# Copying a finished background product out of PSUM on VectorE instead of ScalarE, in the scan of a bidirectional SSD block

## The chip, the cores and the metric

One of the cores of a Trainium2 chip runs the whole program. The metric is the device time of one execution in microseconds (us). Engines are named as in the profile: PE (TensorE, matmul), PEld (its weight loads), DVE (VectorE), ACT (ScalarE), POOL (GpSimd), SP (SyncE, which here only issues DMAs). Names such as L553 are lines of the kernel.

## The reference, cut to what matters

The reference is one encoder block over 1024 tokens and 16 meta tokens, model width 1024, all in float32. The part that bears on the change:

```
u = rmsnorm(h) @ w_in                      # g_val, g_gate, z, x, B, C, dt, gate_conv, gate_ssm
y_conv = silu(layernorm(dwconv(g_val * sigmoid(g_gate)))) @ conv_out_w
y_fwd  = ssd_chunked(x, dt_f, a_f, B, C)             # 4 groups x 8 heads of 64, state 128, chunks of 128 tokens
y_bwd  = flip(ssd_chunked(flip(x), flip(dt_b), a_b, flip(B), flip(C)))
y_ssm  = gated_rmsnorm(y_fwd + y_bwd + d * x, z) @ ssm_out_w
h = h + (sigmoid(gate_conv) * y_conv + sigmoid(gate_ssm) * y_ssm) @ w_o
h = h + (silu(rmsnorm(h) @ w_gate) * (rmsnorm(h) @ w_up)) @ w_down
```

Three products in it don't belong to the scan itself, but are computed while the scan runs: the columns `gate_conv` and `gate_ssm` of `u`, and the first half (rows 0 to 1023) of the product with `ssm_out_w`.

## The kernel before

Every float32 operand of a large product is split in two rounded parts, high and low, and a product is three matmuls per 128 rows of the inner dimension (`mm3_parts`, L201 to L208). Weights are loaded by SP, rounded on ACT (L138) and their low part is made on POOL or DVE (L139), two tiles ahead.

The program has four stages: projections and convolutions (to about 694 us), the scan (about 694 to 1270 us), the remaining products with `ssm_out_w`, `conv_out_w` and `w_o`, and the feed-forward block.

**The scan.** For each of the 4 groups a backward pass (`backward`, L706) makes transposed tiles and the backward states, and 8 forward chunks (`class Chunk`, L750) make the output of 128 tokens each, 32 chunks in all. A string of letters, `SEQ` (L41, used at L909), fixes the order of the steps of three neighbouring chunks: L loads and computes `cb` (L775 to L781), s/S and t/T make the decay masks and their exponentials in two halves of four heads (`select`, `scores`), D, O and C make the outputs and carry the state, M adds and multiplies by the gate (`gated`, L856), N, P and V square, scale and store. Within a chunk the data goes round the engines: DVE masks `cb` (L777, L778), ACT scales it by dt (`gg`, L788), DVE adds the backward part (L790), PE makes the mask sums `ss`, ACT their exponential (`e`, L810), DVE multiplies (L811), PE multiplies by x, DVE adds up (`y`, L843, L849, L860) and multiplies by the gate (L861), ACT squares that (`sz`, L866), POOL makes the root (`rs`), ACT scales (L870).

**The background.** The digits in `SEQ` put background work between these steps (`step_bg`, L665): the generator `background` (L640) first runs 8 blocks of `gate_block` (L544), each of 4 tiles of 128x512, then loads the first half of the normed scan output (`load_vn`, L613: DMA, then ACT `oph` L622, then DVE `opl` L623), and then 16 tiles of the first half of the `ssm_out_w` product. A tile takes 24 matmuls, cut in three pieces (`PARTS`, L37), so that scan steps fit between them. When the last of the 24 is done, the tile is copied from PSUM to the SBUF tile `w512` (two buffers, in the trace `w`): by L553 for the gate blocks and by L656 for the product. SP stores it in DRAM (L554, L657). There are 32 + 16 = 48 such copies.

**The bank.** All matmul outputs of the scan share 8 PSUM banks (`PSB`, L588). At first background tiles rotate over three banks (`mm`, `ss`, `yd`); from step 18 of the first backward pass on (L883, L884) they have the one bank `mm`. From there the first matmul of a background tile can only start when the copy of the tile before has read that bank.

**What sets the order.** Each engine works through its own queue in order. PE's order in the scan is exactly that of the program text (`strict`, `tie`, L187). The order on DVE, ACT, POOL and SP is decided by the framework's scheduler when the program is built.

Of the kernel before, what the change touches and what calls it, by code (L numbers as in the profile page):

```python
# [57 lines left out]
def tile_hybrid_block(  # L58
# [7 lines left out]
    V, S, GP, PE, SP = nc.vector, nc.scalar, nc.gpsimd, nc.tensor, nc.sync  # L66
    x = x[0]
    out = out[0]
# [73 lines left out]
    def next_w(key):  # L142

        while plan and len(ready) < 2:
            k, view, lo = plan.pop(0)
            ready.append((k, load_w(view, lo)))
        k, w = ready.pop(0)
        assert k == key, (k, key)
        return w
# [106 lines left out]
    def proj(wh, wl, j, spans, ps_of=None):  # L256
        for t0, n in spans:
            ps = (ps_of or ps_mm)()
            yield from mm3_parts(ps[:, :n], [wh[:, k, j * P:(j + 1) * P] for k in range(KC)],
                                 [wl[:, k, j * P:(j + 1) * P] for k in range(KC)],  # L260
                                 [h[:, t0:t0 + n] for h in hnh], [h[:, t0:t0 + n] for h in hnl],
                                 PARTS if ps_of else ())
            yield t0, n, ps

    def z_block(b, pool, ps_of, pool_w=2):
        wh, wl = next_w(f"z{b}")
        for i in range(NTT):
            ps = ps_of()
            sl = slice(NM + i * P, NM + (i + 1) * P)
            for k in range(KC):  # L270
                for q_, (a, bb) in enumerate(((hnh[k], wh), (hnh[k], wl), (hnl[k], wh))):
                    PE.matmul(ps[:, :256], lhsT=a[:, sl], rhs=bb[:, k, :], start=(k == 0 and q_ == 0),  # L272
                              stop=(k == KC - 1 and q_ == 2))
            zt = pool.tile([P, 512], F32, name="w512", tag="w512", bufs=pool_w)[:, :256]
            S.activation(out=zt, in_=ps[:, :256], func=AF.Silu)  # L275
            S.dma_start(out=d_sz[b // 2][i, :, (b % 2) * 256:(b % 2 + 1) * 256], in_=zt)
            yield
# [266 lines left out]
    def gate_block(key, b, dst, pool, ps_of, pool_w=2):  # L544
        w = next_w(f"{key}{b}")
        for j in range(2):
            for done in proj(*w, j, SPAN_R, ps_of):
                if done is None:
                    yield
                    continue  # L550
                t0, n, ps = done
                gt = pool.tile([P, 512], F32, name="w512", tag="w512", bufs=pool_w)
                S.copy(out=gt, in_=ps)  # L553
                SP.dma_start(out=dst[2 * b + j, :, t0 - NM:t0 - NM + n], in_=gt)  # L554
                yield

# [39 lines left out]
    def pc():  # L596
        return pb(next(ps_ring))
# [15 lines left out]
    def load_vn(kh):  # L613

        op = []
        for hh in range(2):
            for k in range(KC):
                raw = wts.tile([P, 1024], F32, name="wraw", tag="wraw", bufs=2)[:, :512]
                SP.dma_start(out=raw, in_=d_vn[2 * kh + k // 4][:, k % 4, hh * 512:(hh + 1) * 512])
                h, l = op_tile()  # L620
                w = prm(R_SN, KC * kh + k)
                S.activation(out=h, in_=raw, func=AF.Copy, scale=w)  # L622
                V.scalar_tensor_tensor(out=l, in0=raw, scalar=w, in1=h.bitcast(F32), op0=ALU.mult, op1=ALU.subtract)  # L623
                op.append((h, l))
        return op

    def gemm(op, key, ps_of, parts=()):

        for b in range(4):
            wh, wl = next_w(f"{key}{b}")  # L630
            for hh in range(2):
                for j in range(2):
                    js = slice(j * P, (j + 1) * P)
                    ps = ps_of()
                    yield from mm3_parts(ps, [wh[:, k, js] for k in range(KC)], [wl[:, k, js] for k in range(KC)],
                                         [t[0] for t in op[hh * KC:(hh + 1) * KC]],
                                         [t[1] for t in op[hh * KC:(hh + 1) * KC]], parts)
                    yield 2 * b + j, hh, ps

    def background():  # L640
        for k, i in BGP:
            if k == "z":
                yield from z_block(i, sd, ps_bg, 2)
            else:
                yield from gate_block(k, i, d_gc if k == "gc" else d_gs, sd, ps_bg)
        hn_ctx.close()
        opp_box.append(ctx.enter_context(tc.tile_pool(name="ops", bufs=16, side="right")))
        op = load_vn(0)
        yield
        for done in gemm(op, "s0", ps_bg, PARTS):  # L650
            if done is None:
                yield
                continue
            i, hh, ps = done
            pt = sd.tile([P, 512], F32, name="w512", tag="w512", bufs=2)
            S.copy(out=pt, in_=ps)  # L656
            SP.dma_start(out=d_p[i, :, hh * 512:(hh + 1) * 512], in_=pt)  # L657
            yield

    ps_bg = lambda: pb(next(bg_ring[0]))  # L660
    bg = background()
    bg_acc = [0.0]
    strict[0] = True
# [231 lines left out]
    for f in range(NCK + 1):  # L895
# [3 lines left out]
        if f % NTT == 0:  # L899
# [8 lines left out]
            V=lambda: old and old.store(), b=ahead, e=extra)  # L908
# [16 lines left out]
    def gate(src, i, ts):  # L925
        gt = mg.tile([P, 512], F32, name="mgt", bufs=3)
        SP.dma_start(out=gt, in_=src[i, :, ts])
        S.activation(out=gt, in_=gt, func=AF.Sigmoid)
        return gt
# [64 lines left out]
    for n_, (i, hh, ps) in enumerate(gemm(op, "s1", pc)):  # L994
        ts = halves(hh)
        gt = gate(d_gs, i, ts)
# [7 lines left out]
    for i, hh, ps in gemm(op, "c", pc):  # L1004
        ts = halves(hh)
        gt = gate(d_gc, i, ts)
# [41 lines left out]
    for b in range(4):  # L1048
        wh, wl = next_w(f"o{b}")
        for i in range(NTT):  # L1050
            ps = pc()
# [131 lines left out]
```

## Time and profile before

| what | value |
|---|---|
| time, median of 3 runs | 2297.45 us (2295.74 to 2298.12) |
| time of the profiled execution | 2297.74 us |
| its span, first to last instruction | 2295.9 us |
| mean granted TensorE clock | 0.991 of 2.4 GHz |
| busy over the whole span: PE, DVE, ACT, POOL | 97%, 60%, 33%, 37% |

The profiled execution lies 0.29 us above the median; 1.84 us of its time lie outside its span. A share of busy time is a mean over stages with different limits, so the stage of the scan is read by itself, in stretches of the trace. In a timeline a row is: start in us, duration in us, engine, line, operation, output<-inputs, shapes, count, and in brackets the idle time of that engine before it and what ended it. "PE mm L196 <- ACT w L553" means that a matmul of PE that writes the bank `mm` sat waiting for ACT's copy `w` of L553.

### The profile page before, as it was taken

The page shows a single profiled execution, that of the slowest core. Times are in us where ns is not written, and L with a number is a line of the kernel's source. Part 1 is how long each engine was busy: PE and PEld are TensorE (multiplying, and loading weights), DVE is VectorE, ACT ScalarE, POOL GpSimd, SP SyncE. Part 2 cuts the span into 40 slices and gives each one's busy share as a digit, 9 for nine tenths or more (in the row PEclk, how much of TensorE's full clock was granted, in tenths as well). Part 3 has the DMA queues.
Part 4 walks back from the last instruction along what each step waited for, and adds up shares of the span by engine and source line. Part 5 has one row for each costly group of instructions (what it writes and reads, how often), then busy time and mean ns, then how long its engine had stood idle before and what let it go on. Part 6 is the DMA issues. An engine that isn't in the chain of part 4 may idle for free.

```text
span 2295.9 us, 30987 instructions
## 1 busy us (share of the span) xinstructions
PE 2228.8 (97%) x12103; PEld 1903.6 (83%) x12103; DVE 1383.9 (60%) x1726; ACT 764.4 (33%) x1386; POOL 846.0 (37%) x729
## 2 busy tenths in 40 slices
PE   7999999999999999988999999999999999999998
PEld 7999999999997766665677788998888888888886
DVE  4389898997871587887997664533332333433236
ACT  6333342322322454545555462223111111111112
POOL 3374664821202586867785510111010110101102
PEclk9999999999999999999999999999999999999999
DMA  4222222232236675746753752411111111111111
GB/s 140 85 76 67 83 70 71 86 119 99 89 109 202 195 209 164 226 142 209 229 169 119 241 159 84 147 38 52 41 56 37 55 39 53 55 37 56 37 55 73
DMA packets 223162, 245.29 MB, mean 107 GB/s; under 512 B 19113, under 2 KB 174361, under 8 KB 223017
## 3 DMA queue, kind: packets, MB, share of 16 engines
q1 hardware_dynamic: 210200, 221.89, 31.3%
q10 hardware_dynamic: 12816, 21.44, 2.5%
q8 instruction: 95, 1.56, 0.3%
q14 instruction: 51, 0.41, 0.1%
HBM read 174.23 MB, written 69.04 MB: 106 GB/s over the span
## 4 chain that ended last, share of the span: by engine, by line
PE 48%; DMA 2%; DVE 2%; ACT 1%; POOL 1%; issue 1%; SPq 0%; POOLq 0%; DVEq 0%; ACTq 0%
PE yo L196 11%; PE mm L196 9%; PE ss L196 4%; PE yd L196 4%; PE cb L196 4%; PE yo L1107 3%; PE ss L1107 2%; PE cb L1107 2%; PE yd L1107 2%; DMA wraw<-d_vn 1%; PE mm L1107 1%; PE yo L1058 1%; PE cb L1058 1%; PE ss L1058 1%; PE mm L1058 1%
## 5 line engine op out<-in xcount | busy, mean ns | idle before, releaser
L139 POOL TENSOR_TENSOR wl<-wraw,wh 128x1024 fp32r<-128x1024 f32 (+1 forms) x103 | 249.9, 2436 | 1080.0 <-ACT wh L138 1079.8
L196 PE MATMUL mm<-hnh,wh 128*128 128x352 f32 (+4 forms) x1208 | 410.6, 340 | 14.9 <-ACT w L553 13.5
L196 PE MATMUL mm<-hnh,wl 128*128 128x352 f32 (+4 forms) x1208 | 403.8, 334 | 2.8 <-POOL wl L139 2.8
L196 PE MATMUL mm<-hnl,wh 128*128 128x352 f32 (+4 forms) x1208 | 405.8, 336 | 0.4 <-DVE hnl L378 0.4
L138 ACT CAST wh<-wraw 128x1024 fp32r<-128x1024 f32 (+1 forms) x172 | 175.0, 1042 | 420.3 <-PE yd L1107 175.5
L139 DVE TENSOR_TENSOR wl<-wraw,wh 128x1024 fp32r<-128x1024 f32 x69 | 139.2, 2020 | 252.6 <-ACT wh L138 247.8
L196 PEld LDWEIGHTS mm<-hnh,wh 128*128 128x128 f32 x1208 | 228.3, 189 | 29.9 <-ACT w L553 17.5
L474 DVE SCALAR_TENSOR_TENSOR acc<-ap,pr,acc 128x1024 f32<-128x1024 f32 x192 | 247.5, 1289 | 6.3
L196 PEld LDWEIGHTS mm<-hnh,wl 128*128 128x128 f32 x1208 | 228.3, 189 | 12.9 <-POOL wl L139 3.4
L196 PEld LDWEIGHTS mm<-hnl,wh 128*128 128x128 f32 x1208 | 228.2, 189 | 9.8 <-issue 1.2
L474 DVE SCALAR_TENSOR_TENSOR acc<-xp,pr,acc 128x1040 f32<-128x1040 f32 x120 | 156.6, 1305 | 4.0
L196 PE MATMUL mm<-oph,wh 128*128 128x512 f32 x344 | 139.5, 405 | 11.9 <-ACT w L656 9.9
L272 PE MATMUL mm<-wh,hnh 128*128 128x256 f32 x512 | 144.7, 283 | 5.1 <-ACT w L275 5.1
L272 PE MATMUL mm<-wl,hnh 128*128 128x256 f32 x512 | 144.6, 283 | 0.0
L272 PE MATMUL mm<-wh,hnl 128*128 128x256 f32 x512 | 144.5, 283 | 0.0
L196 PE MATMUL mm<-opl,wh 128*128 128x512 f32 x344 | 137.1, 398 | 3.0 <-DVE opl L623 3.0
L196 PE MATMUL yo<-oph,wh 128*128 128x512 f32 x352 | 139.0, 395 | 0.0
L196 PE MATMUL yo<-opl,wh 128*128 128x512 f32 x352 | 138.9, 395 | 0.0
L196 PE MATMUL yo<-oph,wl 128*128 128x512 f32 x352 | 138.8, 394 | 0.0
L196 PE MATMUL mm<-oph,wl 128*128 128x512 f32 x344 | 136.7, 397 | 0.0
L758 POOL TENSOR_SCALAR_AFFINE_SELECT sel<-adh 128x512 fp32r<-128x512 f32 x128 | 98.7, 792 | 70.8 <-ACT wh L138 41.6
L513 POOL TENSOR_TENSOR tap<-tap 128x1024 f32<-128x1024 f32 x40 | 96.1, 2403 | 34.4 <-ACT tap L509 33.3
(316 smaller groups left out, 4938.8 us busy)
## 6 DMA issues: line engine op xcount, KB each, us to landing
wraw<-in_w_in_dram SPq DMA_DIRECT2D x72, 512.0 KB, 3.7
xc<-d_x SPq DMA_DIRECT2D x64, 256.0 KB, 3.5
wraw<-in_w_gate_dram SPq DMA_DIRECT2D x22, 512.0 KB, 4.7
wraw<-in_w_up_dram SPq DMA_DIRECT2D x22, 512.0 KB, 3.8
wraw<-in_w_down_dram SPq DMA_DIRECT2D x22, 512.0 KB, 3.7
d_x<-xa ACTq DMA_DIRECT2D x16, 520.0 KB, 2.6
d_sz<-w ACTq DMA_DIRECT2D x64, 128.0 KB, 2.1
d_xt<-xt SPq DMA_DIRECT2D x32, 256.0 KB, 3.3
```

The lines of the kernel that those rows point to most:

```text
L138: S.copy(out=h3[:, sl], in_=r3)
L139: (V if lo[i] == "v" else GP).tensor_tensor(out=l3[:, sl], in0=r3, in1=h3[:, sl].bitcast(F32), op=ALU.subtract)
L196: tie(PE.matmul(out_, **kw))
L272: PE.matmul(ps[:, :256], lhsT=a[:, sl], rhs=bb[:, k, :], start=(k == 0 and q_ == 0), stop=(k == KC - 1 and q_ == 2))
L474: V.scalar_tensor_tensor(out=out_ if last else acc, in0=sl(k), scalar=w(k), in1=acc, op0=ALU.mult, op1=ALU.add)
L513: GP.tensor_tensor(out=t, in0=t, in1=part, op=ALU.add)
L758: GP.affine_select(out=dst, in_=hbc(src, self.c, h0, 4, P, P), pattern=[[0, 4], [-1 if back else 1, P]], compare_op=ALU.is_ge, fill=0.0, b ...
L1058: PE.matmul(ps[:, :256], lhsT=a[:, sl], rhs=bb[:, k, :], start=(k == 0 and q_ == 0), stop=(k == KC - 1 and q_ == 2))
L1107: PE.matmul(ps, lhsT=a[:, sl], rhs=bb[:, k, t0:t0 + n], start=(k == 0 and q_ == 0), stop=(k == 1 and q_ == 2))
```

## The change

The two copies move from the queue of ACT to that of DVE. What they copy, the number of copies, the buffers, the DMAs and the order of the matmuls in the scan stay.

```diff
@@ gate_block @@
                 gt = pool.tile([P, 512], F32, name="w512", tag="w512", bufs=pool_w)
-                S.copy(out=gt, in_=ps)
+                V.tensor_copy(out=gt, in_=ps)
                 SP.dma_start(out=dst[2 * b + j, :, t0 - NM:t0 - NM + n], in_=gt)
@@ background @@
             pt = sd.tile([P, 512], F32, name="w512", tag="w512", bufs=2)
-            S.copy(out=pt, in_=ps)
+            V.tensor_copy(out=pt, in_=ps)
             SP.dma_start(out=d_p[i, :, hh * 512:(hh + 1) * 512], in_=pt)
```

Where the scheduler puts them is shown at two of the 48 tiles. In the queues the buffers are numbered; `w_8249` is the 18th tile, whose copy starts at 861.55 us in the trace of before, and `w_9542` the 26th, at 971.74 us.

ACT's queue before, around the 18th tile (`sbh` is the rounded backward state, `gg` the weighted mask of the next chunk, `cch` the rounded C, `bt` a transposed B, `e` the exponential):

```order
L685 CAST sbh<-s_bl 128x512
L788 ACTIVATE gg<-cb,dt 128x128 x4
L691 CAST cch<-cc 128x128
L553 COPY w_8249<-mm 128x512
L726 COPY bt<-tp 128x128
L810 ACTIVATE e<-ss 128x512
```

The copy stood behind the second set of four `gg` of ACT and ahead of the exponential.

DVE's queue around the same tile, where the row with + is new (`y` is the backward output, `s_bl` the low part of the backward state, `ccl` the low part of C):

```order
 L849 TENSOR_TENSOR y_8220<-yo,ea 128x512
 L790 SCALAR_TENSOR_TENSOR gg<-cb,dt,gg 128x128 x4
+L553 COPY w_8249<-mm 128x512
 L686 TENSOR_TENSOR s_bl<-s_bl,sbh 128x512
 L692 TENSOR_TENSOR ccl<-cc,cch 128x128
```

The copy now stands behind DVE's own four `gg`, which read what ACT's four `gg` wrote.

DVE's queue around the 26th tile:

```order
 L790 SCALAR_TENSOR_TENSOR gg<-cb,dt,gg 128x128 x4
 L686 TENSOR_TENSOR s_bl<-s_bl,sbh 128x512
+L553 COPY w_9542<-mm 128x512
 L692 TENSOR_TENSOR ccl<-cc,cch 128x128
 L811 TENSOR_TENSOR e<-e,gg 128x512
```

Here it stands one operation further back, behind `s_bl`. On ACT the copy was removed between the same neighbours as above.

## Rows read from the trace of the kernel before

**Rows 1.** Busy time in two stretches of the scan, before and after about 776 us.
```profile
core 0: us, PE busy (x) PEld busy (x) DVE busy (x) ACT busy (x) POOL busy (x), PEclk, DMA share, GB/s
694.00:776.00 82.00, 80.94 (x359) 62.67 (x358) 20.11 (x30) 25.03 (x51) 25.67 (x27) 1.00 0.66 202
776.00:1270.00 494.00, 459.66 (x2342) 336.06 (x2341) 401.18 (x712) 256.40 (x630) 361.40 (x435) 0.98 0.62 185
```

**Rows 2.** Waits, 694 to 1290 us: us in total, times, longest us.
```profile
ACT sz L866 <- DVE y L861: 99.6, 31, 8.8
...
PE mm L196 <- ACT w L553: 13.5, 11, 3.2
...
PE mm L196 <- ACT w L656: 9.9, 7, 3.1
```

**Rows 3.** Groups by form, 694 to 1270 us: busy us, mean ns of one, idle before.
```profile
L553 ACT COPY w<-mm 128x512 f32<-128x512 f32 x27 | 15.9, 589 | 21.2 <-PE mm L196 16.9 <-issue 4.2
L656 ACT COPY w<-mm 128x512 f32<-128x512 f32 x16 | 9.3, 582 | 6.8 <-PE mm L196 6.8
L700 DVE COPY s_b<-yo 128x512 f32<-128x512 f32 x4 | 2.8, 688 | 11.0 <-PE yo L196 11.0
```

**Rows 4.** Timeline around the copy of the 18th tile.
```profile
860.91 0.40 PE L196 MATMUL mm<-hnh,wl 128*128 128x512 f32 x1
...
861.55 0.61 ACT L553 COPY w<-mm 128x512 f32<-128x512 f32 x1
...
862.02 1.11 DVE L790 SCALAR_TENSOR_TENSOR gg<-cb,dt,gg 128x128 f32<-128x128 f32 x4
...
862.21 0.50 PE L196 MATMUL mm<-hnh,wh 128*128 128x512 f32 x1 [0.91 <-ACT w L553]
...
863.06 0.97 DVE L686 TENSOR_TENSOR s_bl<-s_bl,sbh 128x512 fp32r<-128x512 f32 x1
...
864.94 0.60 ACT L810 ACTIVATE e<-ss 128x512 f32<-128x512 f32 x1 [0.66 <-PE ss L196]
...
865.57 1.07 DVE L811 TENSOR_TENSOR e<-e,gg 128x512 f32<-128x512 f32 x1 [1.34 <-ACT e L810]
```

**Rows 5.** Timeline around the copy of the 26th tile.
```profile
970.00 0.39 PE L196 MATMUL mm<-hnh,wl 128*128 128x512 f32 x1
...
970.42 0.68 DVE L843 TENSOR_TENSOR y<-yo,ea 128x512 f32<-128x512 f32 x1
...
971.01 0.68 DVE L811 TENSOR_TENSOR e<-e,gg 128x512 f32<-128x512 f32 x1
...
971.74 0.61 ACT L553 COPY w<-mm 128x512 f32<-128x512 f32 x1
...
972.98 0.48 PE L196 MATMUL mm<-hnh,wh 128*128 128x512 f32 x1
...
973.25 0.96 DVE L686 TENSOR_TENSOR s_bl<-s_bl,sbh 128x512 fp32r<-128x512 f32 x1
```

**Rows 6.** Timeline: the first and the last of the 18 waits for a copy.
```profile
754.26 0.59 ACT L553 COPY w<-mm 128x512 f32<-128x512 f32 x1 [4.19 <-issue]
...
754.90 0.50 PE L196 MATMUL mm<-hnh,wh 128*128 128x512 f32 x1 [0.28 <-ACT w L553]
...
1268.59 0.57 ACT L656 COPY w<-mm 128x512 f32<-128x512 f32 x1
...
1268.71 0.75 DVE L623 SCALAR_TENSOR_TENSOR opl<-wraw,pr,oph 128x512 fp32r<-128x512 f32 x1 [1.57 <-ACT oph L622]
```

**Rows 7.** Timeline: the first and the last of 13 places without a wait.
```profile
788.70 1.53 DVE L811 TENSOR_TENSOR e<-e,gg 128x512 f32<-128x512 f32 x1
...
790.35 0.47 PE L196 MATMUL mm<-hnh,wh 128*128 128x512 f32 x1
...
1260.92 0.75 DVE L623 SCALAR_TENSOR_TENSOR opl<-wraw,pr,oph 128x512 fp32r<-128x512 f32 x1
...
1261.57 0.41 PE L196 MATMUL mm<-oph,wh 128*128 128x512 f32 x1
```

**Rows 8.** Timeline: a wait of PE at 1007 us.
```profile
1007.09 0.84 PE L196 MATMUL yd<-e,xt 128*64 128x128 f32 x8 [2.02 <-DVE e L811]
```

**Rows 9.** Busy time in the stretch behind that wait, columns as in rows 1.
```profile
1007.45:1010.80 3.35, 3.35 (x13) 2.14 (x9) 3.28 (x8) 0.47 (x1) 0.00 (x0) 0.50 0.68 176
```

## The prediction

> **What bounds the kernel now.** I read the busy time in stretches first. From 776 us to the end of the scan PE is busy for 459.66 of 494 us, so it is idle for 34.3 us; before 776 us it loses only 1.06 of 82 us [rows 1]. In the long stretch VectorE is busy for 401.18 us (81%), ScalarE for 256.40 us (52%): the change takes work from the emptier engine and gives it to the fuller one. The list of waits says what PE's idle time is: 13.5 us in 11 waits for the copies of L553 and 9.9 us in 7 waits for those of L656, 23.4 us in all [rows 2]. So two thirds of what PE loses in the scan hang on the instructions that are moved, and when each copy is done decides the time. The timelines around single copies come last: they show what stands ahead of a copy in ScalarE's queue, and where VectorE is at that moment.
>
> **One copy.** On ScalarE it takes 589 or 582 ns; the nearest row on VectorE, a copy of the same shape out of PSUM, 688 ns [rows 3]. A copy that starts at the same time therefore frees its bank 0.10 us later. In VectorE's queue it takes up less than that: where VectorE reads PSUM and the next operation waits for nothing, starts lie 0.59 us apart (970.42 to 971.01) [rows 5]. The Trainium skill (Perfetto Trace Analysis, Optimizing Scalar/DVE Operations) gives VectorE some 125 ns of overhead per instruction on PSUM; with 512 elements at the 0.96 GHz of VectorE: DVE Perf Modes (Specifications) this makes an estimate of 0.66 us per copy, and the cross-check below would come to 18.5 us by it instead of 16.5. The distance that the trace shows lies below that estimate, and it is used.
>
> **Where the copies now stand.** The start of a copy on VectorE is taken as the later of two times: the last matmul of its tile is done, or the operation ahead of it in VectorE's new queue ends (starts come about 0.07 us before the end of the one ahead, as between 862.02 plus 1.11 and 863.06 [rows 4]). Its end is 0.69 us later. I did this for all 48.
>
> *The first 11 (to 767.6 us).* VectorE is nearly empty there (20.11 us in 82) [rows 1] and reaches each copy before its matmuls are done. Three short waits exist, the first of 0.28 us [rows 6]; each grows by the slower copy, 0.2 us together. If that cover were gone they would cost like the later ones.
>
> *The waits that exist.* At the 18th tile the matmuls end at 861.31, ScalarE copies from 861.55 to 862.16 and PE goes on at 862.21 after 0.91 us of waiting. VectorE ends the four `gg` ahead of the copy at 863.13; the copy would run from 863.06 to 863.75, 1.6 us after ScalarE's [rows 4]. PE's next mask sums, ScalarE's exponential, and VectorE's product `e` come later by that much, and `e` already stood waiting for this chain for 1.34 us [rows 4]: the delay goes round and nothing absorbs it. The same sum at the last wait gives an end at 1269.46 - 0.07 + 0.69 = 1270.08 against 1269.16, 0.92 us later [rows 6]. Over the 18 places, the first and the last of which are those of [rows 6], this adds up to **+18.6 us**; at three of them VectorE would be earlier, by 0.2 to 0.6 us.
>
> *Places without a wait that get one.* At the 26th tile the bank is wanted at 972.98 and ScalarE is done at 972.35; VectorE's `s_bl` ahead of the copy ends at 974.21, so the copy ends at 974.83 and PE loses 1.9 us [rows 5]. There are 13 such places; the first and the last cost 0.55 and 0.77 us [rows 7], together 16.2 us. They can't all be added. They come in five runs of neighbours (789 to 833 us, 943 to 986, 1143, 1166 to 1202, 1261) in which PE drifts ahead of VectorE; once PE has stopped for VectorE, the next of the run is late by that much less. I count each run once, at its largest: 2.0 + 1.9 + 1.0 + 1.7 + 0.8 = **+7.4 us**. For the same reason the existing wait right behind three of the runs (848, 998, 1215 us) keeps less of its growth: 1.7 + 1.9 + 1.3 = **-4.9 us**.
>
> *What ScalarE gets back.* 48 copies leave its queue, but it stands 99.6 us waiting for VectorE's gated product `y` [rows 2]; it has room and is not the engine that the loop of a chunk waits for. Taken at zero. If every one of the 37 copies after 776 us sped the loop up by the queue time that it gives back, about 0.49 us (0.59 less the 0.10 that lie between distance and duration on VectorE too), that would be -18 us, the other end.
>
> *DMAs.* The stores L554 and L657 are issued by SP in order and wait for the copy; loads behind them start later where the copy is later. Counted at zero while those loads are early; if not, it is part of the second rival.
>
> **The sum**: 18.6 + 7.4 - 4.9 = +21.1 us. A cross-check without timelines: 28 of the 37 copies after 776 us stand somewhere in VectorE's run from `cb` to `y`, not right behind `y`, and lengthen this run by 28 x 0.59 = 16.5 us. The profiled execution is 2297.74 us, so 2318.8 us; against the median of 2297.45 it is **2318.5 us**.
>
> **Rivals.**
>
> *Faster.* ScalarE's queue is what holds the copies: they stand behind the square that waits for `y` [rows 2], and VectorE has no such wait. If VectorE, relieved of waiting because ScalarE's `gg` come earlier, took every copy the moment its matmuls end, a wait would be at most 0.78 us and the 18 would come to 9.6 us: 23.4 - 9.6 = 13.8 us less, **2283.6 us**. It decides in favour where VectorE's operation ahead of the copy ends before ScalarE's copy started, which the trace shows at a few places only; at the others `gg` on VectorE comes after `gg` on ScalarE by its nature. Chance 0.10.
>
> *Much slower.* The runs are not absorbed, since a stop of PE delays what VectorE waits for too: 18.6 + 16.2 = 34.8 us, 2332.2 us. On top, after PE had waited 2.02 us the granted clock fell to 0.50 (1.2 of 2.4 GHz) for the 3.35 us read [rows 8, 9]; six more such stretches, each costing half its length, make 10 us: **2342 us**. Late stores that hold up SP's loads would work the same way. For it speaks that PE goes idle for the same engine again and again, against it that VectorE has 19% of the stretch free. Chance 0.22.
>
> *No change.* PE waits for the pace of VectorE's loop in any case, and ScalarE's relief of 0.49 us a copy pays for most of the 0.59 us on VectorE: 28 x 0.10 = 2.8 us, **2300.3 us**. Against it stands the direct dependence at [rows 4]: the copy itself is late there, whatever the loop's pace. Chance 0.13.
>
> **How the numbers follow.** The forecast, 2304 to 2328 us, has a chance of 0.55. A measurement of this kernel can tell about 0.2% (4.6 us) from no change. Faster by more than that is the first rival: 0.10. Within it is most of the third, 0.09. Slower is the forecast, the second rival and the rest of the third: 0.81. The range that should hold the time 8 times in 10 goes from 2296 to 2342 us: it takes in the third rival and most of the second, and leaves out the first.
>
> **What would show it.** In the profile after, the copies are on DVE, 48 of about 690 ns. Right: the waits of PE for `w`, 23.4 us now, come to some 45 us, now put down to DVE; at the 18th and the 26th tile the copy starts 1.5 us or more after its matmuls; PE's busy time outside these waits stays. ScalarE loses 28 us of busy time and its idle time before `sz` grows. The mechanism is wrong if PE's waits for `w` shrink, if they grow but the time does not (they only replaced other waits of PE), or if the time grows at PE's waits for other things, such as `e`, `opl` or a DMA behind a late store. Granted clock well below 0.98 in the scan would put the difference on the second rival.

## The result and the profile after

| | before | after |
|---|---|---|
| median | 2296.66 us (4 runs, 2295.74 to 2298.12) | 2329.31 us (4 runs, 2327.97 to 2331.75) |
| profiled execution | 2297.74 us | 2327.97 us |
| its span | 2295.9 us | 2326.2 us |
| mean granted clock | 0.991 | 0.986 |

The ratio is 1.0143 with an interval of 1.0125 to 1.0160: 32.7 us slower. The forecast was 2318.5 us with a range to 2342, so the side and the range were right, and the forecast itself was 11 us short.

Busy times over the whole span, first of the kernel before, then of the kernel after:

```profile
PE 2228.8 (97%) x12103; PEld 1903.6 (83%) x12103; DVE 1383.9 (60%) x1726; ACT 764.4 (33%) x1386; POOL 846.0 (37%) x729
```

```profile
span 2326.2 us, 30997 instructions
...
PE 2238.8 (96%) x12103; PEld 1912.2 (82%) x12103; DVE 1403.8 (60%) x1774; ACT 742.3 (32%) x1338; POOL 838.6 (36%) x729
```

The span is 30.3 us longer. Of it PE was busy for 2238.8 instead of 2228.8 us with the same 12103 matmuls (+10.0), and idle for 2326.2 - 2238.8 = 87.4 instead of 2295.9 - 2228.8 = 67.1 us (+20.3). So in this pair of profiles there are two things to explain: PE waits longer, and its matmuls take longer. Busy time in the two stretches of the scan, after (columns as in [rows 1]):

```profile
694.00:776.00 82.00, 80.74 (x358) 62.48 (x358) 26.97 (x41) 19.13 (x40) 25.53 (x27) 1.00 0.67 202
776.00:1270.00 494.00, 442.46 (x2223) 323.58 (x2222) 400.07 (x728) 227.81 (x574) 353.80 (x431) 0.95 0.60 177
```

The first stretch is as it was. In the second PE is busy for 442.46 instead of 459.66 of 494 us, at a mean clock of 0.95 instead of 0.98 [rows 1]. It has done 2223 matmuls where before it had done 2342. VectorE is no fuller than before (400.07 against 401.18 us), since the whole loop runs slower. The list of waits after, 694 to 1330 us (us in total, times, longest):

```profile
ACT sz L866 <- DVE y L861: 104.0, 31, 6.3
...
PE mm L196 <- DVE w L656: 23.3, 8, 7.5
PE mm L196 <- DVE w L553: 22.8, 15, 3.7
...
```

PE's waits for a copied tile `w` come to 46.1 us in 23 places; before they were 23.4 in 18, under ScalarE's name [rows 2]. That is 22.7 us more, where its idle time grew by 20.3 in all: the copies are the whole of it, and other waits shrank a little. The copies themselves, after (groups by form, 694 to 1310 us: busy us, mean ns of one, idle before; five of the first 11 copies read another bank and are not in these groups):

```profile
L553 DVE COPY w<-mm 128x512 f32<-128x512 f32 x27 | 18.5, 684 | 23.7 <-PE mm L196 23.7
L656 DVE COPY w<-mm 128x512 f32<-128x512 f32 x16 | 10.9, 681 | 0.1
```

A copy takes 0.68 us, as the nearest row had said [rows 3]. Now the place of a copy. The timeline after, around the 18th tile:

```profile
861.40 0.40 PE L196 MATMUL mm<-hnh,wl 128*128 128x512 f32 x1
...
862.22 1.11 DVE L790 SCALAR_TENSOR_TENSOR gg<-cb,dt,gg 128x128 f32<-128x128 f32 x4
...
863.25 0.68 DVE L553 COPY w<-mm 128x512 f32<-128x512 f32 x1
863.84 0.68 DVE L686 TENSOR_TENSOR s_bl<-s_bl,sbh 128x512 fp32r<-128x512 f32 x1
...
863.98 0.50 PE L196 MATMUL mm<-hnh,wh 128*128 128x512 f32 x1 [2.18 <-DVE w L553]
```

The tile's last matmul ends at 861.80; the copy stands behind the four `gg` and starts 1.45 us later, where ScalarE's had started 0.24 us later [rows 4]. PE waits 2.18 us instead of 0.91. The 24th, 25th and 26th tile, after:

```profile
943.15 0.39 PE L196 MATMUL mm<-hnh,wl 128*128 128x512 f32 x1
...
946.16 0.68 DVE L553 COPY w<-mm 128x512 f32<-128x512 f32 x1
...
946.89 0.50 PE L196 MATMUL mm<-hnh,wh 128*128 128x512 f32 x1 [1.61 <-DVE w L553]
...
959.39 0.40 PE L196 MATMUL mm<-hnh,wl 128*128 128x512 f32 x1
...
963.10 0.50 PE L196 MATMUL mm<-hnh,wh 128*128 128x512 f32 x1 [1.58 <-DVE w L553]
...
973.72 0.39 PE L196 MATMUL mm<-hnh,wl 128*128 128x512 f32 x1
...
975.36 0.68 DVE L553 COPY w<-mm 128x512 f32<-128x512 f32 x1
...
976.63 0.48 PE L196 MATMUL mm<-hnh,wh 128*128 128x512 f32 x1
```

The 24th and 25th tile, where PE had not waited before, now cost 1.61 and 1.58 us. At the 26th the copy starts 1.25 us after the last matmul, and PE, held up twice already, doesn't wait at all. Only four more places got a wait that they did not have before, the 13th, 14th, 39th and 42nd tile:

```profile
791.85 0.50 PE L196 MATMUL mm<-hnh,wh 128*128 128x512 f32 x1 [1.11 <-DVE w L553]
...
807.92 0.50 PE L196 MATMUL mm<-hnh,wh 128*128 128x512 f32 x1 [0.86 <-DVE w L553]
...
1183.30 0.50 PE L196 MATMUL mm<-oph,wh 128*128 128x512 f32 x1 [0.78 <-DVE w L656]
...
1221.60 0.63 PE L196 MATMUL mm<-oph,wh 128*128 128x512 f32 x1 [2.07 <-DVE w L656]
```

The two largest waits are those for the copies of the 33rd and 34th tile. Before, at the same two tiles:

```profile
1091.02 0.50 PE L196 MATMUL mm<-oph,wh 128*128 128x512 f32 x1 [3.13 <-ACT w L656]
...
1107.45 0.50 PE L196 MATMUL mm<-oph,wh 128*128 128x512 f32 x1 [2.61 <-ACT w L656]
```

After, the same places, and what stands ahead of the 34th tile's copy:

```profile
1097.22 0.80 PE L196 MATMUL mm<-oph,wh 128*128 128x512 f32 x1 [5.53 <-DVE w L656]
...
1112.98 0.40 PE L196 MATMUL mm<-oph,wl 128*128 128x512 f32 x1
...
1114.92 1.04 ACT L138 CAST wh<-wraw 128x1024 fp32r<-128x1024 f32 x1 [1.18 <-DMA wraw<-in_ssm_out_w_dram]
...
1116.00 2.04 DVE L139 TENSOR_TENSOR wl<-wraw,wh 128x1024 fp32r<-128x1024 f32 x1 [1.57 <-ACT wh L138]
...
1117.96 0.60 DVE L790 SCALAR_TENSOR_TENSOR gg<-cb,dt,gg 128x128 f32<-128x128 f32 x2
...
1118.50 1.23 DVE L139 TENSOR_TENSOR wl<-wraw,wh 128x1024 fp32r<-128x1024 f32 x1
...
1119.64 0.60 DVE L790 SCALAR_TENSOR_TENSOR gg<-cb,dt,gg 128x128 f32<-128x128 f32 x2
1120.16 0.68 DVE L656 COPY w<-mm 128x512 f32<-128x512 f32 x1
...
1120.90 0.80 PE L196 MATMUL mm<-oph,wh 128*128 128x512 f32 x1 [7.52 <-DVE w L656]
...
1121.91 0.63 PE L196 MATMUL mm<-oph,wl 128*128 128x512 f32 x1
```

The tile was done at 1113.38 and the copy starts at 1120.16. Ahead of it in VectorE's queue stand two halves of a weight tile's low part (L139). The first waits for ScalarE's rounding (L138), and that for the weights' DMA. So the bank is held by a chain that has nothing to do with this tile.

The first matmul behind the wait takes 0.80 us, where before it took 0.50; a following one takes 0.63 us (1121.91), where the same kind took 0.40 ahead of the wait (1112.98). The clock has fallen. The stretches around these two waits, and the sum over the ten half-clock stretches from 776 to 1274 us, after (columns as in [rows 1]):

```profile
1095.70:1102.50 6.80, 5.28 (x15) 4.14 (x16) 3.77 (x9) 2.11 (x4) 1.64 (x3) 0.51 0.60 198
1116.20:1126.40 10.20, 5.50 (x14) 4.33 (x15) 6.29 (x9) 2.24 (x5) 4.09 (x6) 0.51 0.75 241
...
sum 47.60, PE 38.55 PEld 28.55 DVE 26.14 ACT 10.66 POOL 20.76; mean PE 3.85 PEld 2.85 DVE 2.61 ACT 1.07 POOL 2.08
```

Before, one of the five such stretches, and their sum:

```profile
1072.30:1082.50 10.20, 6.76 (x25) 4.00 (x25) 7.08 (x12) 4.22 (x8) 4.03 (x5) 0.50 0.66 214
...
sum 23.80, PE 20.36 PEld 13.90 DVE 16.05 ACT 6.16 POOL 11.92; mean PE 4.07 PEld 2.78 DVE 3.21 ACT 1.23 POOL 2.38
```

At the lower level, 1.2 GHz, the loss in such a stretch is estimated at half of PE's busy time: about 38.55 / 2 = 19.3 us after and 20.36 / 2 = 10.2 before. The 9.1 us between them account for most of the 10.0 us by which PE's busy time grew. The pair of tiles shows it in small: from the restart after the 33rd to that after the 34th it is 1107.45 - 1091.02 = 16.43 us before and 1120.90 - 1097.22 = 23.68 after, 7.25 more. The wait grew by 7.52 - 2.61 = 4.91; the other 2.3 fit the half-clock stretch to 1102.50, whose 5.28 us of busy PE, all of it behind the restart at 1097.22, cost about 2.6.

### The profile page after: what moved, and what is told of

Read it like the earlier page. It is cut to its first block, busy times and chain, and to the rows that moved or that the text cites. A ratio compares the mean times of both kernels' runs of the same rounds, so it can differ in the third digit from the quotient of the medians.

```text
span 2326.2 us, 30997 instructions
## 1 busy us (share of the span) xinstructions
PE 2238.8 (96%) x12103; PEld 1912.2 (82%) x12103; DVE 1403.8 (60%) x1774; ACT 742.3 (32%) x1338; POOL 838.6 (36%) x729
## 4 chain that ended last, share of the span: by engine, by line
PE 78%; POOL 6%; DVE 5%; DMA 3%; issue 3%; ACT 2%; SPq 0%; POOLq 0%; ACTq 0%; DVEq 0%
PE mm L196 30%; PE yo L196 12%; PE ss L196 6%; PE mm L272 6%; PE yd L196 5%; PE cb L196 4%; PE yo L1107 3%; PE ss L1107 2%; PE cb L1107 2%; PE yd L1107 2%; POOL tap L513 2%; PE tp L199 1%; POOL sel L758 1%; PE mm L1107 1%; PE yo L1058 1%
## 5 line engine op out<-in xcount | busy, mean ns | idle before, releaser
L139 POOL TENSOR_TENSOR wl<-wraw,wh 128x1024 fp32r<-128x1024 f32 (+1 forms) x103 | 248.4, 2421 | 1079.5 <-ACT wh L138 1079.2
L138 ACT CAST wh<-wraw 128x1024 fp32r<-128x1024 f32 (+1 forms) x172 | 174.4, 1041 | 419.0 <-PE yd L1107 175.5
L139 DVE TENSOR_TENSOR wl<-wraw,wh 128x1024 fp32r<-128x1024 f32 x69 | 142.4, 2071 | 252.1 <-ACT wh L138 252.1
```

Source lines behind the costliest of these rows:

```text
L138: S.copy(out=h3[:, sl], in_=r3)
L139: (V if lo[i] == "v" else GP).tensor_tensor(out=l3[:, sl], in0=r3, in1=h3[:, sl].bitcast(F32), op=ALU.subtract)
```

## The experiments

Two theories stood against each other. **Theory 1, the place:** on VectorE the copy stands behind operations that end late, so the only bank of the background comes free late and PE waits. **Theory 2, VectorE's time:** VectorE is the fullest engine of a chunk's loop next to PE, and 48 more operations make the loop longer, wherever they stand. The prediction rested on the first for its sum and on the second for its cross-check.

**One phase alone, the gate blocks.**

```diff
-                S.copy(out=gt, in_=ps)
+                V.tensor_copy(out=gt, in_=ps)
```

> Only the 32 copies of the gate blocks (L553) go to VectorE; the 16 of the product (L656) stay on ScalarE. In the profile of the change the last matmul of a tile had slipped by 5.9 us at the 32nd copy and the end of the span by 30.3 us. If the price of a copy is set by its place in VectorE's queue and by what waits there (theory 1), this half costs 4 to 9 us, with PE's waits for w of L553 near 22.8 us as in the change and those of L656 near the 9.9 us of before. If it is VectorE's time that a copy takes up (theory 2), the cost goes by the number of copies after 776 us, 21 of 37: 57% of 32.7 us, about 18.5 us.

Measured: 2304.39 us against 2296.66, ratio 1.0031 (1.0021 to 1.0041). That is 7.7 us for 32 copies, as the first theory had it.

**The other phase alone, the product.**

```diff
-            S.copy(out=pt, in_=ps)
+            V.tensor_copy(out=pt, in_=ps)
```

> Only the 16 copies of the product (L656) go to VectorE; the gate blocks' 32 stay on ScalarE. Theory 1: the rest of the loss, 20 to 28 us, most of it at the first two product tiles (waits of 5.5 and 7.5 us in the change) with half-clock stretches behind them, and in the stretch of the last seven. Theory 2: 16 of 37, 43% of 32.7 us, about 14 us.

Measured: 2320.53 us, ratio 1.0106 (1.0092 to 1.0120), 23.9 us for 16 copies. The waits of PE for `w` in the two runs, first with the gate copies on VectorE, then with those of the product:

```profile
PE mm L196 <- DVE w L553: 23.3, 15, 3.5
PE mm L196 <- ACT w L656: 10.5, 6, 3.4
```

```profile
PE mm L196 <- DVE w L656: 21.3, 7, 6.3
PE mm L196 <- ACT w L553: 15.4, 11, 4.3
```

The parts add up: 7.7 + 23.9 = 31.6 of 32.7 us. A copy of the product costs 1.5 us and one of the gates 0.24, though both take VectorE the same time. So it is not the count of copies on VectorE that sets the cost. In the second run the wait at the 34th tile, 6.3 us, is there without any gate copy on VectorE. The growth of the waits adds up as well: 33.8 and 36.7 us against 23.4 before, 10.4 and 13.3 more, where the change has 22.7.

**Only the copies that came no later on VectorE.** A counter numbers the copies, and twenty of the 48 go to VectorE.

```diff
+ON_V = set(range(1, 12)) | {21, 22, 23, 32, 35, 36, 37, 38, 46}
...
-                S.copy(out=gt, in_=ps)
+                copy_out(gt, ps)
...
-            S.copy(out=pt, in_=ps)
+            copy_out(pt, ps)
```

> 20 of the 48 copies go to VectorE: the first 11, and nine (21 to 23, 32, 35 to 38, 46) that stand in the change right behind the gated product y, where VectorE was to wait for ScalarE anyway. The other 28 stay on ScalarE. Theory 1: -3 to +4 us. Theory 2: nine of the 37 copies after 776 us, 9/37 of 32.7 us, about +8 us.

Measured: 2296.60 us against 2296.66, ratio 1.0000 (0.9990 to 1.0009). Twenty copies on VectorE for nothing: the first theory again. About the second it says little: eleven of the twenty lie ahead of 776 us, where VectorE is nearly empty, and VectorE's busy time rose by only 12.7 us (1383.9 to 1396.6).

**VectorE's time without the bank.** The copies stay on ScalarE. Behind each, VectorE copies the finished tile twice more, from SBUF into a scratch tile that nobody reads.

```diff
                 S.copy(out=gt, in_=ps)
+                for n_ in range(2):
+                    scr = sd.tile([P, 512], F32, name="scr", tag="scr", bufs=1)
+                    V.tensor_copy(out=scr, in_=gt)
```

> All copies stay on ScalarE as before; VectorE gets, for each of the 48 tiles, two copies of w into a scratch tile that nobody reads, behind ScalarE's copy, together about as long as one copy out of PSUM. PE never waits for them. Theory 2 (VectorE's time): 16 to 30 us slower, as in the change. Theory 1 (the bank is freed late): 0 to 8 us slower, with PE's waits for w at 20 to 32 us.

Measured: 2311.82 us against 2296.39, ratio 1.0068 (1.0056 to 1.0081), 15.4 us: between the two expectations. The dose was too large: VectorE's busy time rose by 46.2 us (1383.9 to 1430.1), by the change itself only by 19.9. One extra copy per tile, the same edit without the loop, comes closer to the change.

> All copies stay on ScalarE, and right behind each VectorE makes one more copy of the finished tile, from SBUF into a scratch tile that nobody reads; the outputs are unchanged. Per tile VectorE is given about what the change gives it (its busy time should rise by 20 to 28 us; it rose by 46 with two copies and by 20 in the change), but no bank of PSUM waits for VectorE. Theory 1 (bank freed late, place in the queue): +4 to +10 us on the kernel before, a third of the change at most, waits of PE for w between 23 and 29 us. Theory 2 (VectorE's time in the loop of a chunk): +20 us or more. If two extra copies cost 15.4 us by their time alone, one should cost about 7.7.

Measured: 2303.00 us against 2297.22, ratio 1.0030 (1.0020 to 1.0040), 5.8 us. Its busy times and its waits of PE for `w`:

```profile
PE 2230.9 (97%) x12103; PEld 1903.8 (83%) x12103; DVE 1404.0 (61%) x1774; ACT 764.2 (33%) x1386; POOL 848.0 (37%) x729
```

```profile
PE mm L196 <- ACT w L553: 14.9, 11, 4.3
PE mm L196 <- ACT w L658: 10.1, 6, 3.5
```

VectorE is as busy as in the change (1404.0 and 1403.8 us), PE waits 25.0 us for `w` instead of 46.1, and PE's busy time is 2.1 us over that of before instead of 10.0. The load alone costs a fifth of what the change costs. The extra copies stand behind ScalarE's copy and so elsewhere in VectorE's queue; only the load is that of the change.

**A second bank, copies on ScalarE and on VectorE.** One bank goes from the transposes to the background tiles, so that a tile's first matmul need not wait for the copy of the tile before.

```diff
-    PSB = dict(mm=1, tp=2, yo=2, ss=1, yd=1, cb=1)
+    PSB = dict(mm=2, tp=1, yo=2, ss=1, yd=1, cb=1)
```

> Copies on ScalarE as before; the background tiles get two banks mm instead of one and the transposes tp one instead of two, so that a tile can start while the one before is copied. Theory 1: PE's waits for w (23.4 us) nearly vanish, under 4 us; the time falls by up to 20 us, less what the single bank of the transposes costs, which no run shows so far (-20 to +15 us). It is the reference for the next run.

> Copies on VectorE as in the change, with the same two banks mm and one tp. Theory 1: the bank is free in time on either engine, so it lies within 6 us of the run with two banks and ScalarE, and PE waits under 6 us for w. Theory 2 (VectorE's time): still 16 to 30 us slower than that run, as with one bank.

Measured: 2286.86 us with the copies on ScalarE, ratio to the kernel before 0.9956 (0.9944 to 0.9969), and 2298.08 with them on VectorE, 1.0006 (0.9997 to 1.0015). PE's largest waits in the first of the two:

```profile
PE tp L199 <- ACT vt L878: 8.8, 8, 3.2
PE tp L199 <- ACT bt L726: 6.2, 11, 2.4
```

No wait for `w` is left in either; PE now waits for the one bank of the transposes, and for less. The choice of engine costs 11.2 us here, where it costs 32.7 with one bank: 21.5 us of the change exist only because one bank is reused. The 11.2 missed both expectations. VectorE's time would fit it: its busy time differs by 36.9 us between the two kernels (1385.4 and 1422.3), and 11.2 / 36.9 is 0.30 us of time per us of VectorE. The runs with extra copies gave 15.4 / 46.2 = 0.33 and 5.8 / 20.1 = 0.29. At 0.3 the 19.9 us of the change come to an estimate of 6 us. But this is argued and not shown, for busy time is a poor measure of the load: the same 48 copies raised it by 19.9 us with one bank and by 36.9 with two. Counted by copies, 48 on VectorE cost 11.2 us here and 48 extra ones out of SBUF 5.8. So the bank is worth 21.5 us of the 32.7, VectorE's load about 6, and the 5 between them stay open.

The Trainium skill (Perfetto Trace Analysis, Optimizing Tensor Performance, Matmuls) asks that independent matmul groups rotate through different banks, so that the copy of one lies beside the matmuls of the next. These two runs agree: the rotation is worth 9.5 us with early copies and 31 us with late ones.

**The twenty copies with two banks.**

```diff
+ON_V = set(range(1, 12)) | {21, 22, 23, 32, 35, 36, 37, 38, 46}
...
-    PSB = dict(mm=1, tp=2, yo=2, ss=1, yd=1, cb=1)
+    PSB = dict(mm=2, tp=1, yo=2, ss=1, yd=1, cb=1)
```

> Two PSUM banks for the background tiles (one fewer for the transposes) and the twenty copies on VectorE that were no later there, the others on ScalarE; numbers for the version with two banks and all copies on ScalarE: 2286.9, all on VectorE: 2298.1. If VectorE's time is what is left of the cost with two banks, about 0.3 us per copy after 776 us, of which nine are moved here: 2287 to 2291. If giving ScalarE relief at easy places gains something: below 2285.5, the fastest of all versions. If the order on VectorE shifts everything else (chaotic): anywhere up to 2298.

Measured: 2289.82 us, ratio 0.9970 (0.9961 to 0.9979). It lies where VectorE's time would put it: 2.1 us more than without them, taken from each one's distance to the kernel before (9.5 and 7.4). The two intervals overlap, so the 2.1 us are not clear of noise. No gain from ScalarE's relief appears. The lowest median stays that of two banks and all copies on ScalarE, 9.5 us under the kernel before.

**The weight splits out of the way.** The low parts of the four weight tiles that stood ahead of the late copies are made on GpSimd, with the copies on VectorE, and as a control with the copies on ScalarE.

```diff
-            add_plan(f"{nm}{i}", w, 256 * i, LOB if nm == "s0" else LOC)
+            add_plan(f"{nm}{i}", w, 256 * i, "gg" if nm == "s0" else LOC)
```

> As the change, but the low parts of the four ssm_out weight tiles of the background (L139, two operations each, 2.04 and 1.23 us ahead of the 34th copy in the change) are made on GpSimd instead of VectorE. If the longest waits come from those splits standing ahead of a copy in VectorE's queue and waiting for a weight DMA and ScalarE's rounding, the wait at the 34th tile falls from 7.5 to under 3.5 us and the time by 5 to 12 us against the change. If the place of the splits does not matter, within 3 us of the change. GpSimd may get too full, which would show as waits for sel.

> The control for the run with the low parts of the four s0 weight tiles moved from VectorE to GpSimd: the same move, with the copies left on ScalarE. Together the two give what the copies on VectorE cost where those weight splits do not stand ahead of them. Theory A (the move of the splits is itself bad, GpSimd delivers the low parts late, and the copies then do cost less on VectorE): this control is 15 us or more slower than the kernel before, 2312 or above, so that the copies' share falls below 20 us. Theory B (the move is nearly neutral, and removing one cause of a late copy only shifts PE's wait to the next): control within 8 us of the kernel before, 2289 to 2305, and the copies cost 30 us or more there too.

Measured: 2334.10 us with the copies on VectorE, ratio 1.0161 (1.0147 to 1.0175), and 2306.49 with them on ScalarE, 1.0040 (1.0026 to 1.0054). The move itself costs 9.3 us, a little more than the bound of 2305 in one expectation and less than the 2312 in the other; the copies cost 37.7 - 9.3 = 28.4 us on top, a little less than the 30 that were expected if the splits hardly matter. The waits of PE for `w` with the copies on VectorE, and the matmul behind the 34th tile's copy:

```profile
PE mm L196 <- DVE w L553: 26.6, 15, 5.6
PE mm L196 <- DVE w L656: 20.0, 9, 5.5
```

```profile
1122.87 0.50 PE L196 MATMUL mm<-oph,wh 128*128 128x512 f32 x1 [2.69 <-DVE w L656]
```

They come to 46.6 us, as in the change. The wait at the 34th tile had gone from 7.52 to 2.69 us, as expected, and others grew in its place; the time did not fall by the 5 to 12 us expected with it. By this pair the splits explain where the longest wait stood, and some 4 us (32.7 - 28.4) of the total.

## Why the prediction was right in its side and short in its size

**The copy itself: right.** 0.68 us was measured and 0.69 taken; starts behind one lie 0.59 us apart (863.25 to 863.84), as taken. The Trainium skill's overhead on PSUM (Perfetto Trace Analysis, Optimizing Scalar/DVE Operations), by which the prediction worked out 0.66 us, is not borne out by this distance.

**The first 11 copies: right.** Their three short waits grew by 0.2 us together, as forecast (0.28, 0.28 and 0.50 us before; 0.35, 0.35 and 0.56 after), and PE's busy time before 776 us changed by 0.2 us.

**The terms of PE's waiting: right in the sum.** They gave +21.1 us; PE's idle time over the whole span grew by 20.3, and its waits for `w` went from 23.4 to 46.1 us, where some 45 had been named. At the 18th tile the copy was to start 1.5 us later than ScalarE's and started 1.2 us later, relative to the matmuls. At the 18th and the 26th it fell a little short of the sign set for it, 1.5 us behind the matmuls (1.45 and 1.25). At the 26th, 1.9 us of waiting were forecast and none came, because the two tiles ahead of it had taken 1.61 and 1.58. Runs of neighbours do absorb, as the prediction had it, but not by one stop each: three of the five runs took two stops (1.11 and 0.86, 1.61 and 1.58, 0.78 and 2.07 us) and two took none. That these come to 8.0 us, where 7.4 were forecast, is partly luck. The waits that existed grew by 22.7 - 8.0 = 14.7 us, where 18.6 - 4.9 = 13.7 were forecast, and half of that growth lies at the 33rd and 34th tile, 2.40 and 4.91 us. The prediction names no weight split, itself waiting for a DMA, ahead of a copy.

**The clock: the step that failed.** In the sum it stood at zero, and six more half-clock stretches, 10 us, were put into the second rival with its chance of 0.22. In the scan five more stretches came, 47.6 us in all instead of 23.8; three of the ten were longer than the 3.35 us that the prediction had read [rows 9]. PE's busy time, which was to stay, grew by 10.0 us. The sign that the prediction had set for this rival, a clock well below 0.98 in the scan, came with 0.95. The waiting of the forecast with the clock of the rival is 2318.5 + 10 = 2328.5 us; 2329.3 was measured, a closeness that owes something to chance, as the next paragraphs show.

The row that should have warned was the prediction's own: a wait of 2.02 us followed by a stretch at 0.50 [rows 8, 9]. Waits of that size were what it forecast. Of the 11 waits for `w` of 2 us or more after, nine have a half-clock stretch that begins in them or right behind them. The waits at 863.98 (2.18 us) and 1237.26 (2.54 us) have none, and before, the two waits at the 33rd and 34th tile (3.13 and 2.61 us) had none either. The stretches in which three of these four lie, the first before, the second after:

```profile
1082.60:1229.20 146.60, 137.08 (x716) 102.05 (x715) 132.07 (x240) 82.58 (x205) 115.60 (x137) 1.00 0.63 185
```

```profile
1225.60:1252.40 26.80, 22.02 (x118) 16.16 (x117) 20.17 (x42) 12.73 (x32) 15.74 (x22) 1.00 0.36 103
```

No run here separates the clock from the waiting, so that longer waits bring the lower clock is argued from their places in the trace. In this the two runs with one phase alone don't add up: PE's busy time was 2226.8 and 2232.5 us in them, 2.0 below and 3.7 above that of before, though their medians add up well.

Nor are 10 us of busy time shown to be 10 us of time, because the clock also differs between executions of one kernel. In 52 of the kernel before, its mean over the span went from 0.991 to 0.995; the profiled one had 0.991. A mean lower by 0.004 is some 18 us more at half clock (2 x 0.004 x 2296). Yet the eight executions at 0.991 took 2298.8 us at the median and the seven at 0.995 took 2295.8: only 3 us, a sixth of the 18. With one extra copy a tile, the one at 0.990 took 2308.2 and the two at 0.994 some 2302.1 us, a third. By these shares the 24 us more at half clock in the scan make an estimate of 4 to 8 us of time. The rest of the 11 us by which the forecast fell short stays open.

**The cross-check: right for the wrong reason.** It counted 28 copies at 0.59 us as a longer loop of VectorE, 16.5 us, and agreed with the sum. The run with the same load and no bank at stake cost 5.8 us, about a third of that. Two estimates of different mechanisms agreed by chance.

**ScalarE's relief and the DMAs: zero was right** as far as the runs show. ScalarE stands 104.0 us before `sz` instead of 99.6, and with two banks no gain from twenty copies fewer on it appeared. Its busy time fell by 22.1 us, not by 28: rows that overlap count once. In PE's list of waits none is put down to a DMA, and no run moved the stores alone.

**The rivals.** Against the first stands that no run with copies moved was measurably faster than the one without. The third supposed that PE waits for VectorE's pace anyway; the second bank, which leaves VectorE's work alone and saves 31 us, excludes it. The second had the clock as a cost, and was wrong in letting every place add up: the places without a wait came to 8.0 us, not 16.2.

## What to carry to other kernels

Judge an engine for copying out of PSUM by what stands ahead of the copy in its queue at the moment the bank is wanted, not by how long the copy takes there: the same 0.68 us cost 0.24 us per tile in one phase and 1.5 in the other. Where waits of a few us on TensorE are forecast, put the half-clock stretches that such waits already show in the trace into the sum, and read from several executions what such a stretch costs. If a single bank is reused for one accumulation after another, a second bank makes the choice of the engine matter less (11.2 us instead of 32.7 here); it was worth 31 us with the late copies and 9.5 with the early ones.

## What the runs showed that was not expected

Each added microsecond of VectorE's busy time went with about 0.3 us of time: 0.29 and 0.33 with the extra copies out of SBUF, 0.30 with those out of PSUM and two banks. In the order named, 5.2, 9.4 and 7.2 us of these rises lie ahead of 776 us, where VectorE still has much idle time in the scan; without that part the ratios are 0.39, 0.42 and 0.38. The doubt about busy time as a measure of the load, named above, holds for all of them.

Taking away the cause of the longest wait (7.52 to 2.69 us at the 34th tile) left the total of the waits where it was, 46.1 and 46.6 us. Other copies in the same queue were waited for longer instead, such as that of the 29th tile.
